# Seven half-size products for each third pair of up-projection tiles, and a feed-forward in three chunks

## The chip, the cores and the metric

The kernel runs on one core of a Trainium2 chip. The metric is the device time of one execution in microseconds (us). Five engines work side by side, each on its own list of instructions in a fixed order: TensorE (PE; its weight loads are shown as PEld), VectorE (DVE), ScalarE (ACT), GpSimd (POOL) and SyncE (SP, which here only issues transfers). An instruction whose operands aren't ready holds up all that stand behind it on its engine.

## The reference, cut to what matters

One step of a one-layer decoder for 512 prompt tokens and 64 sample tokens (576 columns in all); all is fp32. Retention and dilated attention share one input projection and one output projection; what the change touches is the feed-forward behind them:

```
h = _rmsnorm(x, norm2_w)
ua, ub = jnp.split(h @ w_up, [D_FF], axis=-1)          # 1024 -> 2 x 2816
buf = jnp.concatenate([conv_s0.astype(ua.dtype), ua], axis=1)
conv = conv_b
for j in range(CONV_W):                                 # 3 taps along the tokens
    conv = conv + buf[:, j:j + T] * conv_w[j]
x = x + (jax.nn.silu(conv) * ub) @ w_down               # 2816 -> 1024
```

## The kernel before, in words

Activations lie transposed: features on the 128 partitions, the 576 tokens along the free axis, worked on in two halves of 288 columns (`H2`). A weight tile is 128 output columns over 1024 inputs, that is eight blocks of 128 x 128.

Each fp32 operand is split in two parts of fp32r, hi and lo, and a product is hi x hi + hi x lo + lo x hi. So for each block `dense` issues three kinds of matmul on two halves: six matmuls of 288 columns. The weights' hi part is a ScalarE copy (`w_split_hi`, L219), the lo part a VectorE subtraction (`w_split_lo`, L229); both are made one tile ahead of TensorE. SyncE loads the raw tiles (L211), up to three in flight.

The feed-forward handles 22 pairs of tiles. Pair `f` is tile `f` of the first half of `w_up` (`ua`, the branch with the convolution) and tile `22 + f` (`ub`, the gate): 16 blocks, 96 matmuls. `up_post` then scales `ua` by the norm (L1130), does the convolution (ScalarE L1134, VectorE L1138 and L1139), SiLU (ScalarE L1141), scales `ub` (L1146), multiplies both (L1149, L1150, on GpSimd except at a half's last pair) and splits the result into `ghi` (L1152) and `glo` (L1154). After 11 pairs, `dense` takes their 11 results through the down projection: 8 output tiles, each summing over the 11 blocks in order, so the newest result is read last. Then the other 11 pairs and their down projection follow. `last_down` does the last output tile in two column parts (L1222), and `last_norm` follows.

The order on each engine is fixed when the kernel is built: streams of Python generators (`Merge`) are interleaved by the costs they yield. `up_post` is a stream of its own beside the stream of matmuls.

Of the kernel before, what the change touches and what calls it, by code (L numbers as in the profile page):

```python
# [18 lines left out]
P = 128  # L19
D = 1024  # L20
NP = 512
NS = 64
# [124 lines left out]
def decoder_step(ctx, tc, a):  # L147
# [33 lines left out]
    chunks = []  # L181
    IN_ORDER = [4 * sec + hp for hp in range(4) for sec in (1, 2, 0)]
    IN_ORDER += [4 * sec + hp for hp in range(4) for sec in (5, 4, 6)]
    IN_ORDER += [12 + hp for hp in range(4)]
    for m in IN_ORDER:
        chunks.append((("in", m, 0), a["w_in"], m, 0, 8))
    for m in range(8):
        chunks.append((("out", m, 0), a["w_out"], m, 0, 8))
    NFH = 11
    for half in range(2):  # L190
        for f in range(half * NFH, (half + 1) * NFH):
            chunks.append((("up", f, 0), a["w_up"], f, 0, 8))
            chunks.append((("up", NF + f, 0), a["w_up"], NF + f, 0, 8))
        for m in range(8):
            k0 = half * NFH
            chunks.append((("down", m, k0), a["w_down"], m, k0, k0 + 6))
            chunks.append((("down", m, k0 + 6), a["w_down"], m, k0 + 6, k0 + 11))
    raw, split = {}, {}
    state = {"load": 0, "use": 0}

    def w_load(upto):
        while state["load"] < min(upto, len(chunks)):
            w_load_part(state["load"], 0, 8)
            state["load"] += 1

    def w_load_part(i, c0, c1):
        _, w, m, k0, k1 = chunks[i]
        if i not in raw:
            raw[i] = wp.tile([P, 8, P], F32, name="wraw", tag="wraw", bufs=3)
        c1 = min(c1, k1 - k0)  # L210
        sp.dma_start(raw[i][:, c0:c1], wsrc(w, m, k0 + c0, k0 + c1))  # L211

    def w_split_hi(i, c0=0, c1=None):
        if i >= len(chunks) or i in split and c0 == 0:
            return
        if i not in split:
            split[i] = [wp.tile([P, 8, P], F32R, name="whi", tag="whi", bufs=2), None]
        c = slice(c0, c1 or chunks[i][4] - chunks[i][3])
        act.activation(split[i][0][:, c], raw[i][:, c], AF.Copy)  # L219

    def w_split_lo(i, c0=0, c1=None):
        if i >= len(chunks) or split[i][1] is not None and c0 == 0:
            return
        if split[i][1] is None:
            split[i][1] = wp.tile([P, 8, P], F32R, name="wlo", tag="wlo", bufs=2)
        hi, lo = split[i]
        n = chunks[i][4] - chunks[i][3]
        c = slice(c0, c1 or n)
        dve.tensor_sub(lo[:, c], raw[i][:, c], f32(hi[:, c]))  # L229
        if c.stop == n:  # L230
            raw.pop(i)

    def w_split(n):
        for i in range(state["use"], n):
            w_split_hi(i)
            w_split_lo(i)

    def w_next(key):
        i = state["use"]
        assert chunks[i][0] == key, (chunks[i][0], key)  # L240
        w_split(i + 1)
        state["use"] += 1
        return i, split.pop(i)

    def dense(ps, key, xhi, xlo, k0, k1, first, last, rows=None, made=None):

        i, (hi, lo) = w_next(key)
        w_split_hi(i + 1)
        for k in range(k0, k1):
            while made is not None and k not in made:  # L250
                yield None
            for wt, x in ((hi, xhi), (hi, xlo), (lo, xhi)):
                for s in range(2):
                    pe.matmul(ps[:, C0 + s * H2:C0 + (s + 1) * H2], wt[:, rows[k] if rows else k - k0], x[k][:, s * H2:(s + 1) * H2],  # L254
                              start=first and k == k0 and wt is hi and x is xhi,
                              stop=last and k == k1 - 1 and wt is lo)
            if k == k0 + 1:
                w_split_lo(i + 1)
            if k == k0 + 3:
                w_load(i + 4)  # L260
            yield 738.0, 0.0
# [167 lines left out]
    def w_first():  # L429
        for i, h in ((0, 0), (1, 0), (0, 1), (1, 1)):  # L430
            w_split_hi(i, 4 * h, 4 * h + 4)
            yield 0.0, 700.0
            w_split_lo(i, 4 * h, 4 * h + 4)
            wk.add((i, h))
            yield 0.0, 900.0
# [3 lines left out]
    def in_first():  # L439
# [5 lines left out]
        for _, _, i, k in steps:  # L445
            while k not in split_k or (i, k // 4) not in wk:
                yield None
            hi, lo = split[i]
            for wt, x in ((hi, xhis), (hi, xlos), (lo, xhis)):
                for s in range(2):  # L450
                    pe.matmul(ps[i][:, C0 + s * H2:C0 + (s + 1) * H2], wt[:, k], x[k][:, s * H2:(s + 1) * H2],  # L451
                              start=k == 0 and wt is hi and x is xhis, stop=k == KD - 1 and wt is lo)
            if k == KD - 1:
                state["use"] += 1
                split.pop(i)
                if i == 0:
                    w_split_hi(2)
                    w_split_lo(2)
# [7 lines left out]
        yield from dense(first[m], ("in", m, 0), xhis, xlos, 0, KD, True, True)  # L466
# [109 lines left out]
    def in_proj():  # L576
        for m in IN_ORDER:
# [3 lines left out]
            else:  # L581
# [3 lines left out]
                for c in dense(ps, ("in", m, 0), xhis, xlos, 0, KD, True, True):  # L585
# [440 lines left out]
    fp = ctx.enter_context(tc.tile_pool(name="ffn", bufs=1, reuse_waits="tile"))  # L1026
    hhi = fp.tile([P, KD, T], F32R, name="hhi")
    hlo = fp.tile([P, KD, T], F32R, name="hlo")
    hhis, hlos = [hhi[:, k] for k in range(KD)], [hlo[:, k] for k in range(KD)]
    acc = fp.tile([P, T], F32, name="acc")  # L1030
    csT = fp.tile([P, NF, 16], F32, name="csT")
    cout = fp.tile([P, 18, NF], F32, name="cout")
    nfw = fp.tile([P, D], F32, name="nfw")
    UE = NP + 2 + B * (TS + 2)
    ss2 = stat[:, 10:15]
# [3 lines left out]
    def sum_squares(m, norm):  # L1039
# [4 lines left out]
        sq = fp.tile([P, T], F32, name="sq", tag="sq", bufs=2)  # L1044
# [23 lines left out]
    h_made, norm2_made, cs_made, up_made, rows_made = set(), [], [], [], set()  # L1068
# [9 lines left out]
    def out_proj():  # L1078
        for m in range(KD):
            ps = dtile()  # L1080
            yield from dense(ps, ("out", m, 0), xhis, xlos, 0, KD, True, True, MIX)
            mg.add(out_post(m, ps))
        yield 0.0, 200.0

    def out_post(m, ps):
            dve.tensor_add(xT[:, m], tok(ps), xT[:, m])
            if m % 4 == 2:
                keep_rows()
            yield 0.0, 900.0
            act.activation(hhi[:, m], xT[:, m], AF.Copy, scale=n2[:, m:m + 1])  # L1090
            yield 0.0, 100.0
            dve.scalar_tensor_tensor(hlo[:, m], xT[:, m], n2[:, m:m + 1], f32(hhi[:, m]), op0=OP.mult,
                                     op1=OP.subtract)
            sum_squares(m, 2)
            h_made.add(m)
            if m == KD - 1:
                while len(h_made) < KD:
                    yield None
                yield 0.0, 3400.0
                yield from norm2()  # L1100
# [14 lines left out]
    def up(f, ghi, glo, made):  # L1115
        pa = dtile()
        yield from dense(pa, ("up", f, 0), hhis, hlos, 0, KD, True, True, made=h_made)
        pb = dtile()
        done = []
        mg.add(up_post(f, pa, pb, done, ghi, glo, made), None, 4000.0 if f == 0 else 0.0)  # L1120
        yield from dense(pb, ("up", NF + f, 0), hhis, hlos, 0, KD, True, True)
        done.append(1)

    def up_post(f, pa, pb, done, ghi, glo, made):
# [8 lines left out]
        c = fp.tile([P, UE], F32, name="cv", tag="cv", bufs=2)  # L1133
# [11 lines left out]
        g = fp.tile([P, T], F32, name="g", tag="g", bufs=2)  # L1145
        dve.tensor_mul(g, tok(pb), rstd_b)  # L1146
        yield 0.0, 1000.0
        eng = dve if f % NFH == NFH - 1 else pool
        eng.tensor_tensor(g[:, :NP], g[:, :NP], c[:, :NP], op=OP.mult)  # L1149
        eng.tensor_tensor(by_seq(g[:, NP:]), by_seq(g[:, NP:]), seqs(c, 0, TS), op=OP.mult)  # L1150
        yield 0.0, 3200.0 if eng is pool else 1000.0
        act.copy(ghi[f % NFH], g)  # L1152
        yield 0.0, 2300.0
        dve.tensor_sub(glo[f % NFH], g, f32(ghi[f % NFH]))  # L1154
        made.add(f % NFH)
        up_made.append(f)
        if f % 2 == 0:
            keep_rows()
# [16 lines left out]
    def rows_out(m, yn):  # L1175
        ps, p2 = mtile(), mtile()
        for j in range(5):
# [4 lines left out]
        dve.tensor_tensor(yn[:, 0:4, c], ps.rearrange("p (j c) -> p j c", j=4),  # L1182
                          nfw[:, None, c].to_broadcast([P, 4, P]), op=OP.mult)
        dve.tensor_tensor(yn[:NS, 4, c], p2[:NS, :P], nfw[:NS, c], op=OP.mult)
        rows_made.add(m)

    def g_tiles(which):
        t = big.tile([P, KD, T], F32R, name="b" + which, tag="b" + which, bufs=1)
        u = fp.tile([P, NFH - KD, T], F32R, name="g" + which, tag="g" + which)
        return [t[:, k] for k in range(KD)] + [u[:, k] for k in range(NFH - KD)]  # L1190

    def down_post(m, ps, half, yn):
        dve.tensor_add(xT[:, m], tok(ps), xT[:, m])
        if half == 1:
# [10 lines left out]
    def last_down(ghi, glo, yn):  # L1205

        m, k0 = KD - 1, NFH
# [4 lines left out]
        for p, (c, tiles) in enumerate(parts):  # L1212
            n = c.stop - c.start
            for k in range(NFH):
                if p == 0 and k in (0, 6):
                    i, (hi, lo) = w_next(("down", m, k0 + k))
                    w += [(hi[:, x], lo[:, x]) for x in range(min(6, NFH - k))]
                    if k == 0:
                        w_split_hi(i + 1)
# [112 lines left out]
```

## Time and profile before

| | us |
|---|---|
| median of 3 runs | 829.08 (828.67 to 830.43) |
| the profiled execution's own time | 830.02 |
| its span, first to last instruction | 828.2 |
| TensorE busy | 809.3 (98%) |
| VectorE busy | 413.4 (50%) |
| ScalarE busy | 294.4 (36%) |
| GpSimd busy | 148.0 (18%) |

The profile is of one execution; its own time stands 1.8 us above its span and 0.9 us above the median of the runs. A matmul's shown duration overlaps with that of the next, so how fast TensorE works is read from a long unbroken piece of the chain divided by its matmuls.

### The profile page before, as it was taken

To read this page: it belongs to the slowest core of one execution; us is meant where nothing else is said; L and a number is where in the kernel's file an instruction comes from. 1 tells how busy PE (TensorE), PEld (TensorE's weight loads), DVE (VectorE), ACT (ScalarE), POOL (GpSimd) and SP (SyncE) were. 2 spreads that over 40 slices of the span, in tenths; PEclk is the share of its full clock that TensorE was granted. 3 is DMA by queue.
4 is the path that set the end of the run, shared out by engine and by line. 5 is a ranking of instruction groups with operands and counts; after the bars stand their busy time and mean duration, and the time that the engine had idled before them with its cause. 6 is when DMAs were issued, how large, how long until landed. Compare 5 with 4: busy or idle time off the path is not lost.

```text
span 828.2 us, 15913 instructions
## 1 busy us (share of the span) xinstructions
PE 809.3 (98%) x6559; PEld 772.3 (93%) x6559; DVE 413.4 (50%) x792; ACT 294.4 (36%) x503; POOL 148.0 (18%) x240
## 2 busy tenths in 40 slices
PE   7999999999999999999999999999999999999995
PEld 5999999887887888999999999999999999999995
DVE  4664555665546566743545545432245545443333
ACT  5422222454535567433223323311123323332222
POOL 1321202111110213032122322100012322310111
PEclk9999999999999999999999999999999999999998
DMA  9354753678786863456255554443334455543213
GB/s 265 105 175 115 213 173 101 184 210 226 213 254 185 228 177 91 111 185 197 77 179 178 178 187 160 124 137 91 96 99 161 145 153 179 172 160 93 71 52 115
DMA packets 179798, 128.67 MB, mean 155 GB/s; under 512 B 14976, under 2 KB 176400, under 8 KB 179213
## 3 DMA queue, kind: packets, MB, share of 16 engines
q1 hardware_dynamic: 178573, 93.75, 40.4%
q10 hardware_dynamic: 928, 33.63, 11.3%
q8 instruction: 52, 0.85, 0.4%
q0 software_dynamic: 224, 0.28, 0.1%
q14 instruction: 21, 0.17, 0.1%
HBM read 121.52 MB, written 39.66 MB: 195 GB/s over the span
## 4 chain that ended last, share of the span: by engine, by line
PE 93%; ACT 3%; DVE 1%; issue 1%; DMA 1%; POOL 0%; SPq 0%; ACTq 0%; DVEq 0%
PE d L254 74%; PE m L883 2%; PE d L451 2%; PE m L928 1%; PE d L893 1%; PE m L810 1%; PE m L797 1%; PE m L496 1%; PE m L1222 1%; PE px L254 1%; PE m L666 1%; DMA wraw<-in_w_in_dram 1%; ACT s L786 1%; PE m L630 1%; PE px L410 1%
## 5 line engine op out<-in xcount | busy, mean ns | idle before, releaser
L219 ACT ACTIVATE whi<-wraw 128x1024 fp32r<-128x1024 f32 (+2 forms) x114 | 110.5, 970 | 369.2 <-issue 182.6
L229 DVE TENSOR_TENSOR wlo<-wraw,whi 128x1024 fp32r<-128x1024 f32 (+2 forms) x114 | 127.1, 1115 | 121.7 <-ACT whi L219 118.9
L254 PE MATMUL d<-bhi,whi 128*128 128x288 f32 x768 | 172.7, 306 | 1.2 <-DVE t L557 1.2
L254 PE MATMUL d<-bhi,wlo 128*128 128x288 f32 x768 | 164.2, 295 | 0.0
L254 PE MATMUL d<-blo,whi 128*128 128x288 f32 x768 | 163.9, 295 | 0.0
L254 PE MATMUL d<-hhi,whi 128*128 128x288 f32 x704 | 151.0, 296 | 0.0
L254 PE MATMUL d<-hlo,whi 128*128 128x288 f32 x704 | 150.8, 296 | 0.0
L254 PE MATMUL d<-hhi,wlo 128*128 128x288 f32 x704 | 150.7, 296 | 0.0
L254 PEld LDWEIGHTS d<-bhi,whi 128*128 128x128 f32 x768 | 121.7, 189 | 6.3 <-issue 3.1
L254 PEld LDWEIGHTS d<-bhi,wlo 128*128 128x128 f32 x768 | 123.3, 188 | 0.0
L254 PEld LDWEIGHTS d<-blo,whi 128*128 128x128 f32 x768 | 123.2, 188 | 0.0
L254 PEld LDWEIGHTS d<-hhi,whi 128*128 128x128 f32 x704 | 113.5, 189 | 0.1
L254 PEld LDWEIGHTS d<-hhi,wlo 128*128 128x128 f32 x704 | 113.5, 189 | 0.0
L254 PEld LDWEIGHTS d<-hlo,whi 128*128 128x128 f32 x704 | 113.5, 189 | 0.0
L1130 DVE TENSOR_TENSOR ue<-d,rstd_b 128x512 f32<-128x512 f32 x22 | 15.2, 691 | 74.5 <-PE d L254 74.5
L1149 POOL TENSOR_TENSOR g<-g,cv 128x512 f32<-128x512 f32 x20 | 25.8, 1289 | 142.2 <-DVE g L1146 136.7
L791 POOL TENSOR_SCALAR s<-s,sc 128x128 f32<-128x128 f32 (+3 forms) x32 | 17.3, 549 | 140.5 <-DVE sc L789 125.9
L1046 POOL TENSOR_TENSOR acc<-acc,sq 128x576 f32<-128x576 f32 x13 | 20.9, 1611 | 104.2 <-ACT sq L1045 104.2
L1135 POOL COPY cout<-ue 128x2 f32<-128x2 f32 x22 | 5.7, 260 | 137.6 <-DVE ue L1130 137.6
L884 ACT COPY kt<-m 128x384 f32<-128x384 f32 x32 | 15.3, 479 | 38.4 <-PE m L883 36.2
L883 PE MATMUL m<-ident,kc 128*128 128x128 f32 x192 | 27.4, 277 | 0.8 <-DVE sc L779 0.7
L884 DVE COPY kt<-m 128x384 f32<-128x384 f32 x32 | 17.8, 556 | 19.4 <-PE m L883 19.0
(269 smaller groups left out, 1027.3 us busy)
## 6 DMA issues: line engine op xcount, KB each, us to landing
wraw<-in_w_up_dram SPq DMA_DIRECT2D x44, 512.0 KB, 4.7
wraw<-in_w_in_dram SPq DMA_DIRECT2D x26, 512.0 KB, 3.8
kc<-in_cache_win_k_dram SPq DMA_DIRECT2D x32, 256.0 KB, 4.8
vc<-in_cache_win_v_dram SPq DMA_DIRECT2D x32, 256.0 KB, 3.2
wraw<-in_w_down_dram SPq DMA_DIRECT2D x16, 384.0 KB, 4.0
wraw<-in_w_down_dram SPq DMA_DIRECT2D x16, 320.0 KB, 3.2
kc<-in_cache_win_k_dram SPq DMA_DIRECT2D x64, 64.0 KB, 3.4
vc<-in_cache_win_v_dram SPq DMA_DIRECT2D x64, 64.0 KB, 3.3
```

Of the source, the lines that this page charges most:

```text
L219: act.activation(split[i][0][:, c], raw[i][:, c], AF.Copy)
L229: dve.tensor_sub(lo[:, c], raw[i][:, c], f32(hi[:, c]))
L254: pe.matmul(ps[:, C0 + s * H2:C0 + (s + 1) * H2], wt[:, rows[k] if rows else k - k0], x[k][:, s * H2:(s + 1) * H2], start=first and k == k ...
L410: pe.transpose(ps[:, s], xn[:r, j, k * P:(k + 1) * P], ident[:r, :r])
L451: pe.matmul(ps[i][:, C0 + s * H2:C0 + (s + 1) * H2], wt[:, k], x[k][:, s * H2:(s + 1) * H2], start=k == 0 and wt is hi and x is xhis, stop ...
L496: pe.transpose(p1[:, j * P:(j + 1) * P], src[:, j * P:(j + 1) * P], ident)
L791: pool.tensor_scalar(s[:, :n], s[:, :n], c[:, 2:3], 1.0, op0=OP.mult, op1=OP.mult)
L883: pe.transpose(ps[:, j * P:(j + 1) * P], K[u, x][:, 3 * w + j], ident)
L884: (act.copy if w else dve.tensor_copy)(kt[:, w * 384:w * 384 + 384], ps[:, :384])
L1046: pool.tensor_tensor(acc, acc, sq, op=OP.add)
L1130: dve.tensor_mul(u[:, 2:NP + 2], ya[:, :NP], rstd_b[:, :NP])
L1149: eng.tensor_tensor(g[:, :NP], g[:, :NP], c[:, :NP], op=OP.mult)
```

## The change

Of the 22 pairs, seven (`f` = 2, 5, 8, 11, 14, 17, 20) are now done as a product of 2 x 2 blocks in Winograd's form of Strassen's scheme: the weights' block rows are `ua` and `ub` and their block columns are inputs 0 to 511 and 512 to 1023, the activations' blocks are those two input halves by the two token halves. Seven products of 4 blocks by 288 columns take the place of eight: 7 x 4 x 3 = 84 matmuls for 96.

The activations' sums T1 to T4 are made and split once, in `out_post`, beside the output projection, whose tiles come in the order 0, 4, 1, 5 ... for that. The weights' sums S1 to S4 are made on VectorE for each of the seven pairs, from four quarters ahead (`sums`), and each is split like a weight. The products' results are put together on VectorE with copies that ScalarE takes out of PSUM (`ct`, `g`).

Weights are now split in quarters of a pair (up to four blocks), two to three quarters ahead, not a tile at a time; the next raw tile is loaded when one is used up. The feed-forward goes in three chunks of 6, 8 and 8 pairs, each followed by its part of the down projection. GpSimd's part in the gate goes to VectorE for all pairs. The final norm's weight is loaded behind the last pair.

```diff
-    NFH = 11
-    for half in range(2):
-        for f in range(half * NFH, (half + 1) * NFH):
-            chunks.append((("up", f, 0), a["w_up"], f, 0, 8))
-            chunks.append((("up", NF + f, 0), a["w_up"], NF + f, 0, 8))
+    CHUNKS = [(0, 6), (6, 14), (14, 22)]
+    SEVEN = set(range(2, NF - 1, 3))
...
+    def add_slab(f):
...
+        quarters.extend([(i, slice(0, 4)), ("S1", f), (i, slice(4, 8)), ("S2", f), ("S4", f), (i + 1, slice(4, 8)),
+                         ("S3", f)])
+        reads[i], reads[i + 1] = 5, 3
+        for n, which in ((-4, "S1"), (-3, "S2"), (-2, "S4"), (-1, "S3")):
+            sums.setdefault(j + n, []).append((which, f, i))
...
+    def ahead_of():
+        return 3 if state["ffn"] else 2
+    def w_begin(j):
+        for which in sums.pop(j, []):
+            w_sum(*which)
+        while state["hi"] <= min(j + ahead_of(), len(quarters) - 1):
+            if state["lo"] < state["hi"]:
+                w_lo(state["lo"])
+                state["lo"] += 1
+            w_hi(state["hi"])
+            state["hi"] += 1
...
+    def up_seven(f, n, ghi, glo, made):
...
+        order = ((pa, "B11"), (pc, "T1"), (pb, "B21"), (pa, "T2"), (pc, "B22"), (pd, "T4"), (pa, "T3"))
+        for q, (dst, c) in enumerate(order):
...
+            for k in range(4):
+                while c[0] == "T" and (c, k) not in t_made:
+                    yield None
+                for wt, b in ((hi, xh), (hi, xl), (lo, xh)):
+                    pe.matmul(dst, wt[:, k], b[:, k], start=q in (0, 1, 2, 5) and k == 0 and wt is hi and b is xh,
+                              stop=k == 3 and wt is lo, skip_group_check=True)
...
+            if q == 0:
+                act.copy(ts[0], pa)
+            elif q == 1:
+                act.copy(ts[1], pc)
+            elif q == 2:
+                dve.tensor_tensor(y[:, :H2], pb, ts[0], op=OP.add)
+            elif q == 3:
+                act.copy(ts[2], pa)
+            elif q == 4:
+                dve.tensor_tensor(y[:, H2:T], pc, ts[2], op=OP.add)
+                mg.add(post_seven(f, n, pa, ts[1], y, z, stage, ghi, glo, made))
+            elif q == 5:
+                act.copy(z[:, :H2], pd)
...
+    def post_seven(f, n, pa, t, y, z, stage, ghi, glo, made):
...
+        dve.tensor_mul(u[:, 2:NP + 2], y[:, :NP], rstd_b[:, :NP])
...
+        act.activation(c[:, :L], u[:, 0:L], AF.Identity, scale=convw[:, 0, f:f + 1], bias=convb[:, f:f + 1])
...
+        dve.tensor_tensor(z[:, :H2], pa, z[:, :H2], op=OP.add)
+        dve.tensor_tensor(z[:, H2:T], pa, t, op=OP.add)
+        yield 0.0, 900.0
+        dve.scalar_tensor_tensor(c[:, :L], u[:, 1:L + 1], convw[:, 1, f:f + 1], c[:, :L], op0=OP.mult, op1=OP.add)
+        dve.scalar_tensor_tensor(c[:, :L], u[:, 2:L + 2], convw[:, 2, f:f + 1], c[:, :L], op0=OP.mult, op1=OP.add)
...
+        dve.tensor_mul(z[:, :T], z[:, :T], rstd_b)
...
+        yield from gated(f, n, z, c, ghi, glo, made)
```

The two orders on TensorE. In the up projection before, in any pair: each weight block serves the two token halves, in two PSUM banks.

```order
L254 MATMUL d<-hhi,whi 128x288 x2
L254 MATMUL d<-hlo,whi 128x288 x2
L254 MATMUL d<-hhi,wlo 128x288 x2
L254 MATMUL d<-hhi,whi 128x288 x2
L254 MATMUL d<-hlo,whi 128x288 x2
```

Now, in one of the seven pairs, at the end of its first product and in its second (`T` is a sum of activations):

```order
L1262 MATMUL m<-hhi,whi 128x288
L1262 MATMUL m<-hlo,whi 128x288
L1262 MATMUL m<-hhi,wlo 128x288
L1262 MATMUL m<-T,whi 128x288 x2
L1262 MATMUL m<-T,wlo 128x288
L1262 MATMUL m<-T,whi 128x288 x2
```

The 288-column matmuls stand in groups of three to one bank now, not of six to two; 12 fewer of them make up a pair.

VectorE's order where the first chunk of the feed-forward ends and its down projection begins. Before, from the `ub` of pair 10, the last of its half, to the first output tile of the down projection:

```order
L1146 TENSOR_TENSOR g<-d,rstd_b 128x576
L1149 TENSOR_TENSOR g<-g,cv 128x512
L1150 TENSOR_TENSOR g<-g,cv 128x64
L229 TENSOR_TENSOR wlo<-wraw,whi 128x768
L1154 TENSOR_TENSOR glo<-g,ghi 128x576
L1193 TENSOR_TENSOR xT<-d,xT 128x576
```

Now, from where the last product of pair 5, the last of its chunk, can be read (L1295) to the first output tile (L1377); two splits of weights, not shown, stand right ahead:

```order
L1295 TENSOR_TENSOR g<-m,g 128x288
L1296 TENSOR_TENSOR g<-m,ct 128x288
L296 TENSOR_TENSOR wlo<-wraw,whi 128x384
L1298 SCALAR_TENSOR_TENSOR cv<-ue_4471,vec,cv 128x592
L1299 SCALAR_TENSOR_TENSOR cv<-ue_4471,vec,cv 128x592
L1302 TENSOR_TENSOR g<-g,rstd_b 128x576
L1308 TENSOR_TENSOR g<-g,cv 128x512
L1309 TENSOR_TENSOR g<-g,cv 128x64
L1313 TENSOR_TENSOR blo<-g,bhi 128x576
L296 TENSOR_TENSOR wlob<-wraw,whib 128x384
L1377 TENSOR_TENSOR xT<-d,xT 128x576
```

Between the last matmul of the chunk's last pair and its last result (`glo`, `blo`) stood five instructions; now nine stand there, and the pair's two convolution steps are among them.

## Rows read from the trace of the kernel before

**Rows 1.** The page's head and its part 1: busy time.
```profile
span 828.2 us, 15913 instructions
PE 809.3 (98%) x6559; PEld 772.3 (93%) x6559; DVE 413.4 (50%) x792; ACT 294.4 (36%) x503; POOL 148.0 (18%) x240
```

**Rows 2.** Busy time by stretch (us; then PE, PEld, DVE, ACT, POOL, granted clock, DMA).
```profile
440.00:480.00 40.00, 40.00 (x302) 40.00 (x301) 18.57 (x24) 12.79 (x16) 9.40 (x15) 1.00 0.55 172
800.00:828.00 28.00, 19.47 (x148) 18.61 (x146) 9.22 (x27) 7.15 (x10) 3.12 (x3) 0.90 0.23 85
```

**Rows 3.** The chain that ended last, in order of time (start us, us, what).
```profile
400.18 349.44 PE d L254 x2622
...
809.59 1.76 PE m L1222 x12
...
816.78 2.16 PE m L1222 x18
```

**Rows 4.** Groups of VectorE by form, 340 to 828 us (busy us, mean ns | idle before).
```profile
L229 DVE TENSOR_TENSOR wlo<-wraw,whi 128x1024 fp32r<-128x1024 f32 x51 | 62.5, 1225 | 64.6 <-ACT whi L219 62.6
...
L1138 DVE SCALAR_TENSOR_TENSOR cv<-ue,vec,cv 128x592 f32<-128x592 f32 x22 | 18.1, 823 | 0.0
L1146 DVE TENSOR_TENSOR g<-d,rstd_b 128x576 f32<-128x576 f32 x22 | 16.5, 750 | 0.0
...
L1130 DVE TENSOR_TENSOR ue<-d,rstd_b 128x512 f32<-128x512 f32 x22 | 15.2, 691 | 74.5 <-PE d L254 74.5
...
L1131 DVE TENSOR_TENSOR ue<-d,rstd_b 128x64 f32<-128x64 f32 x22 | 4.7, 214 | 0.0
...
L1237 DVE TENSOR_TENSOR xT<-m,xT 128x320 f32<-128x320 f32 x1 | 0.5, 490 | 3.6 <-PE m L1222 3.6
...
L1237 DVE TENSOR_TENSOR xT<-m,xT 128x256 f32<-128x256 f32 x1 | 0.4, 425 | 0.8 <-PE m L1222 0.8
```

**Rows 5.** Groups by form over the whole span: the smallest splits.
```profile
L229 DVE TENSOR_TENSOR wlo<-wraw,whi 128x512 fp32r<-128x512 f32 x4 | 2.8, 688 | 2.9 <-ACT whi L219 2.9
...
L219 ACT ACTIVATE whi<-wraw 128x512 fp32r<-128x512 f32 x4 | 2.5, 631 | 5.8 <-DMA wraw<-in_w_in_dram 5.8
```

**Rows 6.** Groups of ScalarE by form, 340 to 828 us.
```profile
L219 ACT ACTIVATE whi<-wraw 128x1024 fp32r<-128x1024 f32 x51 | 54.0, 1060 | 207.1 <-issue 150.2 <-PE d L254 56.8
L1134 ACT ACTIVATE cv<-ue,vec 128x592 f32<-128x592 f32 x22 | 19.4, 880 | 5.7 <-DVE ue L1131 5.5
L1141 ACT ACTIVATE cv<-cv 128x592 f32<-128x592 f32 x22 | 15.0, 683 | 2.9 <-DVE cv L1139 2.9
...
L1152 ACT CAST bhi<-g 128x576 fp32r<-128x576 f32 x16 | 10.5, 657 | 0.0
...
L1283 ACT ACT_TABLE_LOAD x1 | 1.3, 1283 | 0.0
```

**Rows 7.** Timeline of VectorE in one pair (start us, us, line).
```profile
449.62 0.75 DVE L1154 TENSOR_TENSOR blo<-g,bhi 128x576 fp32r<-128x576 f32 x1
450.29 0.82 DVE L1138 SCALAR_TENSOR_TENSOR cv<-ue,vec,cv 128x592 f32<-128x592 f32 x1
```

**Rows 8.** Timeline of ScalarE in the same pair.
```profile
448.35 0.66 ACT L1152 CAST bhi<-g 128x576 fp32r<-128x576 f32 x1
448.91 0.88 ACT L1134 ACTIVATE cv<-ue,vec 128x592 f32<-128x592 f32 x1
```

**Rows 9.** Timeline of VectorE and TensorE where the first down projection begins.
```profile
537.13 0.75 DVE L1154 TENSOR_TENSOR glo<-g,ghi 128x576 fp32r<-128x576 f32 x1
...
538.57 0.43 PE L254 MATMUL d<-ghi,whi 128*128 128x288 f32 x2
```

**Rows 10.** Timeline of TensorE, first matmuls of the span.
```profile
9.92 0.85 PE L451 MATMUL d<-blo,whi 128*128 128x288 f32 x2
...
14.93 0.42 PE L451 MATMUL d<-blo,whi 128*128 128x288 f32 x2
```

**Rows 11.** Busy time by stretch, columns as in rows 2: the end of the span.
```profile
822.00:824.00 2.00, 0.00 (x0) 0.00 (x0) 0.92 (x2) 1.15 (x1) 0.00 (x0) 0.65 0.81 217
```

More of the change, by code (lines that the diff above doesn't have):

```diff
@@ L233, in w_split, with w_read @@
[L233 to L261, printed above, removed]
+    def w_read(i):
+        reads[i] -= 1
+        if not reads[i]:
+            raw.pop(i)
+        if state["auto"]:
+            while state["load"] < len(raws) and len(raw) < (4 if state["ffn"] else 3):
+                w_load(state["load"] + 1)
@@ new lines, in w_hi, with w_lo @@
+    def w_hi(j):
+        if j < len(quarters) and j not in split:
+            src = w_src(j)
+            n = src.shape[1]
+            split[j] = [w_tile("whi", j), None]
+            act.activation(split[j][0][:, :n], src, AF.Copy)
+    def w_lo(j):
+        if j < len(quarters) and split[j][1] is None:
+            src = w_src(j)
+            n = src.shape[1]
+            split[j][1] = w_tile("wlo", j)
+            dve.tensor_sub(split[j][1][:, :n], src, f32(split[j][0][:, :n]))
+            x, c = quarters[j]
+            if isinstance(x, str):
+                S.pop((x, c))
+                if x == "S3":
+                    w_read(quarters[keys["seven", c]][0] + 1)
+            else:
+                w_read(x)
@@ new lines, in dense @@
+    def dense(ps, key, xhi, xlo, k0, k1, first, last, made=None):
+        j, k = keys[key], k0
+        while k < k1:
+            w_begin(j)
+            if split[j][1] is None:
+                w_mid(j)
+            hi, lo = split.pop(j)
+            c = quarters[j][1]
+            for x in range(c.stop - c.start):
+                while made is not None and k not in made:
+                    yield None
+                for wt, b in ((hi, xhi), (hi, xlo), (lo, xhi)):
+                    for s in range(2):
+                        pe.matmul(ps[:, C0 + s * H2:C0 + (s + 1) * H2], wt[:, x],
+                                  b[k][:, s * H2:(s + 1) * H2],
+                                  start=first and k == k0 and wt is hi and b is xhi,
+                                  stop=last and k == k1 - 1 and wt is lo)
+                if x == 0:
+                    w_mid(j)
+                k += 1
+                yield 738.0, 0.0
+            j += 1
@@ L1144, in up_post @@
         yield 0.0, 1400.0
-        g = fp.tile([P, T], F32, name="g", tag="g", bufs=2)
-        dve.tensor_mul(g, tok(pb), rstd_b)
+        g = tmp("g")
+        dve.tensor_mul(g[:, :T], tok(pb), rstd_b)
         yield 0.0, 1000.0
[L1148 to L1158, printed above, removed]
+        yield from gated(f, n, g, c, ghi, glo, made)
     def conv_state_out():
@@ L1290, in feed_forward @@
                 ps = dtile()
[L1291 to L1294 removed]
+                yield from dense(ps, ("down", m, f0), ghi, glo, 0, f1 - f0, True, True, made=made)
+                mg.add(down_post(m, ps, last, yn))
     mg.add(conv_state_in(), None)
```

314 lines of the change are left out of this document (209 added, 105 removed).

## The prediction

> **What bounds the kernel now.** I read the page's head first: TensorE is busy for 809.3 of 828.2 us, VectorE for half the span [rows 1]. Of the 18.9 us that are left, 8.5 us lie in the last 28 us, where little but the final norm is left to do [rows 2]; 10.4 us are all the rest, the start of the span included. The chain of waits then has one unbroken piece of 349.44 us of nothing but the matmuls of `dense`, from the first pairs through the first down projection to the second [rows 3]. So in the feed-forward TensorE is the limit: a matmul less is time off the kernel, and any moment for which TensorE waits is time on it. In a middle stretch of 40 us of it VectorE works 18.57 us and ScalarE 12.79 us [rows 2]; both have room, VectorE less.
>
> **What a matmul costs.** 349.44 us over 2622 matmuls is 133.3 ns for 288 columns [rows 3]. The new order writes one PSUM bank at a time, with hi, hi, lo of a block behind each other. That pattern is there already, in `last_down`: 12 matmuls of 320 columns in 1.76 us (147 ns) and 18 of 256 in 2.16 us (120 ns) [rows 3]. Half-way between lies 133.3 ns, so I take the same price. Taken away are 7 x 12 = 84 matmuls: **-11.2 us**.
>
> **What VectorE and ScalarE get on top.** A split of 512 elements takes VectorE 688 ns against 1225 ns for one of 1024 [rows 4, 5], ScalarE 631 against 1060 ns [rows 5, 6]. Sums of weights are not in the trace; the nearest row is the 512-element subtraction, which reads two tiles in SBUF too, so 688 ns. An addition of 288 columns out of PSUM lies between 425 ns (256) and 490 ns (320) [rows 4]: 457 ns. For ScalarE's copies of 288 columns I take 440 ns, from 631 ns less 224 elements at the slope of its two splits.
>
> A pair of the old kind then costs VectorE 4 splits (2.75), the scaling of `ua` (0.69 + 0.21), two convolution steps (0.82 each), the scaling of `ub` (0.75), the gate (about 0.69 + 0.21, as the scaling of `ua` has these shapes) and `glo` (0.75): 7.7 us beside 12.8 us of TensorE. One of the seven costs 7 splits (4.82), 4 sums (2.75), 4 half additions (1.83) and the same 4.95 us: 14.35 us beside 84 x 0.1333 = 11.2 us. Alone it is too much; over two old and one new it is 29.8 us in 36.8 us. All hangs on whether the surplus can move to the neighbours.
>
> I walked the order of both engines through such pairs, each instruction starting when its engine and its operands are free. Operations that don't depend on each other overlap by about 0.08 us on VectorE (450.29 is less than 449.62 + 0.75) and 0.1 us on ScalarE (448.91 is less than 448.35 + 0.66) [rows 7, 8]. Weights are split three quarters ahead, 4.8 us of these products. In pair 2, where the activations' sums have delayed VectorE most (it gets to the scaling of pair 1's `ua` 1.3 us late), the walk has every split ready over 2 us before its matmul; in the other pairs over 1.7 us. The copies out of `pa`, which must end before TensorE adds to it again, come about 2 us early. So between the pairs I cost all this at **0**; if the cover were gone, the first to be late would be the lo part of a product's weights, and each microsecond of it would be one on the chain.
>
> The split T sums (32 half-size operations on VectorE, some 15 us) lie beside the output projection and pairs 0 and 1, 77 us of TensorE: **0**. In front of the feed-forward the quarter splits add 26 x 0.15 us on VectorE and 26 x 0.2 us on ScalarE in 330 us, but let ScalarE wait less for TensorE's buffers; of TensorE's matmuls there the order is unchanged. I take **0**, with bounds of 2 us each way, a fifth of the 10.4 us of idle time. Eight more additions to `xT` for the third down projection (750 ns each at most) lie beside 6 blocks of matmuls each: 0. The final norm's weight, now loaded late, has 6.4 us of matmuls as cover.
>
> **The new wait.** The down projection reads the newest pair last. Before, pair 10 stood behind ten others: `glo` ended at 537.88 and its first matmuls began at 538.57 [rows 9], 0.7 us to spare. The first chunk has 6 pairs, so its newest result is due after 5 blocks of 6 matmuls, 4.0 us, and that pair, 5, is one of the seven: everything behind its last product starts only then. My walk, in us from the start of its first product; the last one ends at 11.2, readable at 11.4:
>
> ScalarE: cast of pair 4 5.9 to 6.5, hi of S3 to 7.1, copy of `pa` to 7.4, two hi parts for down (384 elements, 0.52 each) to 8.3, `cv` (after the scaled `ua`) 10.6 to 11.5, copy of `pd` to 11.8, three more hi parts to 13.1.
> VectorE: lo of S3 7.1 to 7.8, `glo` of pair 4 to 8.5, a lo part (384, 0.55) to 8.9, second `y` addition to 9.3, lo to 9.8, scaled `ua` to 10.6, two lo parts 12.3 to 13.3, two `z` additions to 14.1, lo to 14.5, convolution to 16.2 (its second step waits for the first), scaling of `z` to 16.8, gate 16.9 to 17.7; ScalarE's cast to 18.4; `glo` 18.45 to 19.2.
>
> TensorE would have begun this block at 15.2 and needed `glo` two matmuls later, at 15.47: it waits **3.8 us**. Bounds: were nothing else in the queues, from 11.4 on two additions, convolution, scaling, gate, cast and `glo` end at 17.0, a wait of 1.5 us; with every duration in full and no overlap the walk ends at 21.0, a wait of 5.5 us. I take 3.8, as rows 7 and 8 show the overlap. VectorE's section on the drain in the Trainium skill (VectorE: DVE Perf Modes, "The DRAIN you can't avoid") has an operation start only when the pipe behind the one before is empty, unless it isn't held; by its first half the time would be that of the 5.5 us, and the overlap in rows 7 speaks for its second.
>
> The second chunk ends with two old pairs: the same walk has its last `glo` 3.9 us behind the last matmul, due after 7 blocks, 5.6 us. The third ends with an old pair behind a new one, with two table loads of ScalarE (1.28 us each [rows 6]) in the way: 5.5 us, due at 5.6 us. Both **0** (bound 1.2 us for the third).
>
> **Sum.** 828.2 - 11.2 + 3.8 = 820.8 us of span; 830.02 - 7.4 = 822.6 us for the profiled execution, whose own time is 0.94 us above the median of the runs, so **821.7 us** for the median. The gap's bounds give 819.4 to 823.4; the front's 2 us and the third end's 1.2 us widen that to 817.4 to 826.6.
>
> **Rivals.**
> *VectorE becomes the bound (slower).* If the surplus of each new pair can't move, TensorE waits in each for 14.35 - 11.2 = 3.2 us: 7 x 3.2 = 22 us, 829.1 - 11.2 + 22 + 3.8 = 843.7 us; with the overlap of 0.08 us on 20 operations it is 1.55 us each, 832.6 us. It decides from waits of (11.2 - 3.8) / 7 = 1.06 us per pair on. For it: 14.35 against 11.2 us, and a VectorE that waits in order for copies and products. Against it: 29.8 in 36.8 us over three pairs, and sums that start four quarters ahead. Chance 0.11.
> *The clock falls in the wait (824 to 826 us).* In 822 to 824 us, with no matmul running, the granted clock's mean is 0.65 of the 2.4 GHz, which is a fall to the lower level of 1.2 GHz on the way [rows 11]; behind the idle start two matmuls took 0.85 us against 0.42 us later, from 9.9 to some time before 14.9 us [rows 10]. At half pace for 5 to 9 us, TensorE would lose 2.5 to 4.5 us. Our wait of 3.8 us is the only one that long. The Trainium skill (TensorE: Matmul & The Clock Gate, "HAM oscillation — how this bites in real kernels") says that TensorE is throttled again in such idle gaps between matmuls; by that rule the time would be this rival's. The trace shows it only where all work was over. Chance 0.12.
> *The products run slower.* If a change of weights at each third matmul cost more than shown, 588 matmuls at 146 ns would eat all (89.6 - 3.8 = 85.8 us over 588). Rows 3 stand against it: at 256 columns the same pattern runs at 120 ns. Chance 0.03, some 829 us.
> *No wait at the first chunk's end, or a faster front (816 to 818.5 us).* Chance 0.06.
>
> My forecast has the remaining 0.68. Range 818 to 826.5 us. A measurement of this kernel tells about 0.2% (1.7 us) from no change: faster 0.85, within 0.07, slower 0.08, the last from the first and third rivals.
>
> **What would show it.** TensorE's matmuls of `up_seven`: 588, in unbroken pieces at 133 ns, 11.2 us a pair. One idle gap of 2 to 5 us on TensorE, ended by ScalarE's cast or VectorE's `blo`, some 4 us behind the end of pair 5; none above 1 us at the ends of the other chunks. VectorE busy for over 60% between the first new pair and the last. I am wrong if TensorE waits for `wlo` in several of the seven pairs, if the pace within them is not 133 ns, or if the clock drops behind the gap.

## The result, and the profile after

| | before | after |
|---|---|---|
| median of 6 runs each, us | 829.69 (828.67 to 831.05) | 840.09 (839.43 to 845.11) |
| after / before, 95% interval | | 1.0142 (1.011 to 1.0174) |
| span of the profiled execution, us | 828.2 | 843.2 |
| mean granted clock of TensorE in it | 0.997 | 0.985 |

The change made the kernel slower by 10.4 us where 7.4 us less were forecast. The profiled execution took 845.11 us at a granted clock of 0.985, as two of the six do; the other four took 839.4 to 840.1 us at 0.989. So what is read from the profile below holds for an execution 5 us above the median.

The head of the page after, with busy time and the granted clock in 40 slices, answers to [rows 1]:

```profile
span 843.2 us, 16199 instructions
PE 806.4 (96%) x6475; PEld 767.5 (91%) x6475; DVE 504.2 (60%) x1064; ACT 338.7 (40%) x670; POOL 100.8 (12%) x200
PEclk9999999999999999999999989999999999999997
```

TensorE is busy for 2.9 us less than before, not 11.2, and idle for 36.8 us instead of 18.9. So there are two things to find: 18 us of new waits, and 8.3 us by which the same matmuls ran slower.

Who TensorE waited for, over the whole span (us in total, times, longest):

```profile
PE px L486 <- DMA vrows<-in_norm_w_dram: 5.5, 1, 5.5
PE m L883 <- POOL s L877: 4.7, 4, 2.7
PE d L337 <- ACT bhi L1311: 3.2, 1, 3.2
PE d L337 <- DVE t L643: 2.6, 1, 2.6
PE m L969 <- DVE sc L865: 2.3, 3, 1.3
PE m L1148 <- POOL acc L1141: 2.1, 1, 2.1
PE d L337 <- DVE g L1341: 1.6, 1, 1.6
PE d L979 <- DVE t L649: 1.3, 1, 1.3
```

The first row is the start, as before. L1311 is the gap at the first chunk's end, forecast at 3.8 us; L1141 and L1341 stand at the feed-forward's beginning. All the others (`s`, `t`, `sc`: operations of the attention) lie in front of it, from 150 to 350 us, where TensorE's waits add up to 13.4 us against 4.0 before. That part of the program was forecast at 0.

A landmark shows the same: the squares of the output projection's columns (ScalarE). Before, and after:

```profile
L1045 ACT ACTIVATE sq<-xT x7: 669/673/674, 350.8 to 389.5; 128x576 f32<-128x576 f32 x7
```

```profile
L1140 ACT ACTIVATE sq<-xT x7: 666/669/672, 367.6 to 409.5; 128x576 f32<-128x576 f32 x7
```

They begin 16.8 us later than before and end 20 us later.

The granted clock, by stretch (columns as in [rows 2]):

```profile
168.80:172.20 3.40, 3.40 (x24) 1.50 (x17) 1.21 (x3) 0.00 (x0) 0.00 (x0) 0.50 0.61 159
...
243.90:247.30 3.40, 3.40 (x18) 3.38 (x17) 0.56 (x1) 0.67 (x2) 0.52 (x4) 0.50 0.56 143
271.20:274.60 3.40, 3.21 (x14) 3.04 (x15) 1.46 (x5) 0.65 (x2) 0.48 (x2) 0.50 0.18 53
489.60:496.40 6.80, 5.91 (x23) 5.62 (x24) 2.58 (x5) 1.62 (x3) 0.00 (x0) 0.50 0.28 80
```

Four stretches at 1.2 instead of 2.4 GHz, 17 us in all, each at or behind one of the longer waits: 17 / 2 = 8.5 us, about the 8.3 us that busy TensorE lost. Before, there was none between the start and the end of the work.

The new pairs themselves, and the first chunk's end, in the chain of waits, in order of time:

```profile
435.71 11.10 PE m L1262 x84
446.82 25.41 PE d L337 x192
472.23 10.99 PE m L1262 x83
...
489.76 0.68 ACT bhi L1311
...
490.49 62.77 PE d L337 x450
553.26 11.14 PE m L1262 x84
```

Seven times 84 matmuls in 11.1 us, with nothing between them and their neighbours: this part is as forecast. VectorE's last result of pair 5 comes behind the cast:

```profile
490.47 0.76 DVE L1313 TENSOR_TENSOR blo<-g,bhi 128x576 fp32r<-128x576 f32 x1 [0.74 <-ACT bhi L1311]
```

**The account of the profiled execution**, from the forecast span of 820.8 us: waits in front of the feed-forward 13.4 - 4.0 = 9.4; three half-clock stretches there 3 x 1.7 = 5.1; 1.9 us in the first 18 us, where two matmuls took 0.68 us and more until 18.1 us (before, 0.42 us at 14.9 us [rows 10]), by the lines below; two waits at the feed-forward's beginning 3.7; half clock behind the gap 3.4; the gap 3.2 instead of 3.8. That is 843.7; the span is 843.2 us.

The same matmuls near the start, before and after:

```profile
16.25 0.80 PE L410 MATMUL px<-ident,xn 128*128 128x128 f32 x5
```

```profile
17.66 0.68 PE L535 MATMUL d<-bhi,wlo 128*128 128x288 f32 x2
18.14 1.03 PE L494 MATMUL px<-ident,xn 128*128 128x128 f32 x5
```

### The profile page after: what moved, and what is told of

The parts are those of the page before. It is cut to its first block, busy times and chain, and to the rows that moved or that the text cites. A ratio compares the mean times of both kernels' runs of the same rounds, so it can differ in the third digit from the quotient of the medians.

```text
span 843.2 us, 16199 instructions
## 1 busy us (share of the span) xinstructions
PE 806.4 (96%) x6475; PEld 767.5 (91%) x6475; DVE 504.2 (60%) x1064; ACT 338.7 (40%) x670; POOL 100.8 (12%) x200
## 3 DMA queue, kind: packets, MB, share of 16 engines
q10 hardware_dynamic: 928, 33.63, 11.1%
## 4 chain that ended last, share of the span: by engine, by line
PE 48%; DVE 1%; ACT 1%; issue 0%; POOL 0%; ACTq 0%; DVEq 0%; POOLq 0%
PE d L337 37%; PE m L1262 9%; PE m L1407 1%; PE m L1364 0%; ACT yn L1453 0%; DVE wlo L296 0%; PE m L1387 0%; POOL acc L1141 0%; PE m L1148 0%; DVE T L1184 0%; ACT whi L289 0%; ACT cv L1329 0%; DVE cv L1299 0%; DVE yn L1448 0%; DVE g L1341 0%
## 5 line engine op out<-in xcount | busy, mean ns | idle before, releaser
L296 DVE TENSOR_TENSOR wlo<-wraw,whi 128x512 fp32r<-128x512 f32 (+1 forms) x149 | 107.8, 729 | 88.7 <-ACT whi L289 87.8
L337 PEld LDWEIGHTS d<-bhi,whi 128*128 128x128 f32 x784 | 125.8, 191 | 11.1 <-ACT bhi L1311 3.4
L289 ACT ACTIVATE whi<-wraw 128x512 fp32r<-128x512 f32 (+1 forms) x149 | 90.3, 619 | 70.0 <-PE d L337 47.3
L337 PE MATMUL d<-hhi,whi 128*128 128x288 f32 x400 | 85.2, 294 | 1.6 <-DVE g L1341 1.6
L337 PE MATMUL d<-hlo,whi 128*128 128x288 f32 x400 | 85.4, 295 | 0.0
L337 PE MATMUL d<-hhi,wlo 128*128 128x288 f32 x400 | 85.3, 294 | 0.0
L337 PEld LDWEIGHTS d<-hhi,whi 128*128 128x128 f32 x400 | 63.9, 188 | 1.9 <-ACT whi L289 1.8
L337 PEld LDWEIGHTS d<-hhi,wlo 128*128 128x128 f32 x400 | 63.9, 188 | 0.0
L337 PEld LDWEIGHTS d<-hlo,whi 128*128 128x128 f32 x400 | 63.7, 187 | 0.0
L1377 DVE TENSOR_TENSOR xT<-d,xT 128x576 f32<-128x576 f32 x23 | 17.4, 757 | 39.9 <-PE d L337 39.9
L1262 PE MATMUL m<-T,whi 128*128 128x288 f32 x168 | 33.9, 295 | 0.0
L1330 POOL COPY cout<-ue 128x2 f32<-128x2 f32 x15 | 11.1, 739 | 185.4 <-DVE ue L1325 185.4
L1311 ACT CAST bhi<-g 128x576 fp32r<-128x576 f32 x22 | 14.8, 674 | 44.3 <-DVE g L1309 44.3
L1141 POOL TENSOR_TENSOR acc<-acc,sq 128x576 f32<-128x576 f32 x13 | 19.3, 1487 | 102.7 <-ACT sq L1140 102.7
```

The lines of the kernel that those rows point to most:

```text
L289: act.activation(split[j][0][:, :n], src, AF.Copy)
L296: dve.tensor_sub(split[j][1][:, :n], src, f32(split[j][0][:, :n]))
L337: pe.matmul(ps[:, C0 + s * H2:C0 + (s + 1) * H2], wt[:, x], b[k][:, s * H2:(s + 1) * H2], start=first and k == k0 and wt is hi and b is xh ...
L1141: pool.tensor_tensor(acc, acc, sq, op=OP.add)
L1262: pe.matmul(dst, wt[:, k], b[:, k], start=q in (0, 1, 2, 5) and k == 0 and wt is hi and b is xh, stop=k == 3 and wt is lo, skip_group_chec ...
L1311: act.copy(ghi[n], g[:, :T])
```

## The theory, and its rivals

**Why the front is late.** The attention's operations on VectorE are not slower (`t` takes 0.75 us in both traces); they stand behind something. Who VectorE waited for from 150 to 345 us, as to `wlo`, the weights' lo part. Before:

```profile
DVE wlo L229 <- ACT whi L219: 2.0, 3, 0.8
```

After:

```profile
DVE wlo L296 <- ACT whi L289: 14.7, 15, 1.6
```

One of the fifteen, in the timelines of ScalarE, VectorE and TensorE:

```profile
166.31 0.63 ACT L289 ACTIVATE whi<-wraw 128x512 fp32r<-128x512 f32 x1
...
166.97 0.69 DVE L296 TENSOR_TENSOR wlo<-wraw,whi 128x512 fp32r<-128x512 f32 x1 [1.61 <-ACT whi L289]
167.58 0.75 DVE L649 TENSOR_TENSOR t<-d,rstd_b 128x576 f32<-128x576 f32 x1
...
168.39 1.60 PE L979 MATMUL d<-kt,qb 128*32 128x512 f32 x8 [1.33 <-DVE t L649]
```

ScalarE comes to `whi` only behind four casts of the attention. VectorE reaches `wlo` 1.61 us too early and stands; `t`, whose operands are ready, stands behind it; TensorE waits 1.33 us for `t`, and the clock falls. Before, hi and lo of a tile were issued at a dense's start and behind its second block; after, the lo part follows one block behind its hi part, and there are twice as many.

Theory A: the distance of lo from hi in the queues (A1 in experiment 2). Rivals: the number of splits (B); the hi parts' place on ScalarE (A2). For the rest: the gap of 3.2 us comes of a new pair read last, and the clock falls because of the gap; the two waits at the feed-forward's beginning come of the T sums and of the added copy in `out_post`.

## The experiments

All times are medians of device time; the kernel before has 829.6 to 830.1 us beside them.

**1. Both parts in the places of before** (`front_order`)

```diff
     def w_begin(j):
...
-        while state["hi"] <= min(j + ahead_of(), len(quarters) - 1):
-            if state["lo"] < state["hi"]:
+        if not state["ffn"] and j % 2:
+            return
+        while state["hi"] <= min(j + 3, len(quarters) - 1):
+            if state["ffn"] and state["lo"] < state["hi"]:
...
-                if x == 0:
+                if x == (0 if state["ffn"] else 1):
                     w_mid(j)
...
```

> In front of the feed-forward the half-size weight splits are issued in the places of before (both hi parts at a dense's start, both lo parts behind its second block); all else is the changed kernel. Theory A (the new places of the splits in ScalarE's and VectorE's queues make the attention part late): the feed-forward starts within 5 us of before instead of 17 us behind it, TensorE's waits from 150 to 350 us fall from 13.4 us to under 6 us, and with them most of the three 3.4 us stretches at half clock go; 840.1 - 9 - 4 = about 827 us (824 to 831). Rival B (it is the number of splits, twice as many, whatever their place): waits stay over 10 us, 837 to 841 us. The gap at the first chunk's end stays 3.2 us in both.

Measured: 831.4 us, ratio 1.001 (0.9997 to 1.0024), just above the expected 824 to 831 us. The first square starts at 351.0 us (before 350.8), the waits from 150 to 350 us are 3.9 us, and no half-clock stretch is left in front. Run again beside experiment 10:

> The kernel with the splits in front in the places of before once more, beside the filled gap: 831.4 us (829.5 to 832.5) with a gap of 3.1 us near 475 us and a stretch of 3.4 or 6.8 us at half clock behind it.

Measured: 829.5 us, ratio 1.0003 (0.9991 to 1.0015), gap 3.13 us, 3.4 us at half clock from 475.5 us. B is out: there are as many splits as in the changed kernel.

**2. The lo parts alone** (`front_lo_later`)

```diff
-                if x == 0:
+                if x == (0 if state["ffn"] else 2):
                     w_mid(j)
```

> The changed kernel with one thing moved: in front of the feed-forward VectorE's lo parts are issued behind the third block of a half instead of behind the first; ScalarE's hi parts stay where the change has them, a half at a time. Theory A1 (VectorE, which works in order, stands at a lo part until ScalarE has made the hi part issued just before it, 14.7 us in 15 waits from 150 to 345 us, and the attention's work stands behind it): these waits go, TensorE's waits in 150 to 350 us fall from 13.4 to under 5 us, and the time comes to that of the run with both parts in the places of before, 831 us (829 to 833). Theory A2 (the hi parts' new place on ScalarE does as much): TensorE still waits for 7 us or more there, 835 to 840 us.

Measured: 831.6 us, 1.001 (0.9998 to 1.0023); TensorE's waits from 150 to 350 us 4.6 us, and of VectorE's waits from 150 to 345 us this is left:

```profile
DVE wlo L296 <- ACT whi L289: 0.9, 2, 0.5
```

A1 holds: two blocks more between hi and lo give 8.5 us back. ScalarE's order needs no change.

**3. Chunks that end with an old pair** (`chunks_7_7_8`)

```diff
-    CHUNKS = [(0, 6), (6, 14), (14, 22)]
+    CHUNKS = [(0, 7), (7, 14), (14, 22)]
```

> Chunks (0,7), (7,14), (14,22) in place of (0,6), (6,14), (14,22), so that each ends with a pair of the old kind; all else is the changed kernel. Theory A (the gap comes of a new pair read last, and the clock falls because of the gap): no wait over 1 us at the first chunk's end and no half-clock stretch behind it; 840.1 - 3.2 - 3.4 = 833.5 us. Rival B (the clock falls for another reason): the 6.8 us at half clock stay, 836.9 us. Rival C (the next-to-last pair being new only moves the wait): 839 to 841 us.

Measured: 836.8 us, 1.0086 (1.0064 to 1.0107). The time is the one that rival B gave; the trace speaks for A: no wait stands between 428 and 820 us, and no half clock. The gain of 3.3 us is half of what was expected from the profiled execution; that most runs of the changed kernel had less half clock to give back may be why (0.989 against 0.985 of 840 us is an estimated 3.4 us, which would leave the gap's own 3.2 us). Where the clock fell in those runs isn't seen.

**4. Both** (`front_order_chunks_7_7_8`)

> Both edits at once. If they act in different places their gains add: about 827 - 6.6 = 820.5 us (817 to 825), faster than before by about 1%. Rival: with the front early again another engine or a transfer is late in the feed-forward; over 828 us.

Measured: 825.8 us, 0.9942 (0.9921 to 0.9964). The gains add (831.4 - 825.8 = 5.6, and 836.8 - 825.8 = 11.0 us), but the median is above the expected range: the waits of 2.1 and 1.6 us at the feed-forward's beginning are still there, with 3.4 us at half clock between them.

**5. No pair by seven products, no T sums** (`no_seven_no_sums`)

```diff
-    SEVEN = set(range(2, NF - 1, 3))
+    SEVEN = set()
...
-        h1 = hs.pop(k)
...
-        yield from h_split("T3", k, b12)
+        hs.pop(k)
```

> No pair by the seven products (all 22 pairs by dense) and none of the T sums; splits by halves, leads, chunks and gate are those of the changed kernel. Leaves nothing out of the result. Theory A (the seven products save 84 matmuls at 133 ns as forecast, 11.2 us, and the T sums cost the 3.7 us of waits in the first two pairs, and the gap with its half clock needs a new pair at the chunk's end): 840.1 + 11.2 - 3.7 - 6.6 = 841 us, waits in front of the feed-forward as in the changed kernel. Rival B (the new pairs or the T sums are what made it slower): 830 us or less.

Measured: 843.3 us, 1.0152 (1.0125 to 1.0179). The waits in front are those of the changed kernel (the same rows, the same 2.7 and 2.6 us); from 350 to 830 us TensorE never waits. So neither the products nor their sums made the front late, and both waits at the feed-forward's beginning go with the sums. The added copy in `out_post` is still in this kernel, so by itself it makes neither wait. Its feed-forward pays the 84 matmuls back: 840.1 + 11.2 - 3.7 - 3.2 - 1.7 (a half-clock stretch of 3.4 us) = 842.7.

**6. Squares first** (`squares_first`, on 4)

```diff
+        sum_squares(m, 2)
         h = hs[m] = tmp("h")
         act.activation(hhi[:, m], xT[:, m], AF.Copy, scale=n2[:, m:m + 1])
         act.activation(h[:, :T], xT[:, m], AF.Copy, scale=n2[:, m:m + 1])
...
         h_made.add(m)
-        sum_squares(m, 2)
```

> The kernel with the splits in the places of before and chunks of 7, 7, 8, and in it ScalarE's square for the norm's sum issued ahead of the two scaled copies of a column instead of behind them. Theory (the added fp32 copy of 0.76 us, with the other ahead of it, makes GpSimd's last addition and so the sums on TensorE late): the wait of 2.06 us for GpSimd's addition near 397 us falls to about 0.6 us, and the 3.4 us at half clock behind it may go: 825.8 - 1.5 = 824.3, without the half clock 822.6 us. Rival (VectorE's late residual addition sets it): the wait stays above 1.5 us, 825 to 826 us.

Measured: 820.0 us, **0.9869 (0.9853 to 0.9886)**. The wait for GpSimd's addition is gone, and the half clock. The gain, 5.8 us, is more than the 2.1 + 1.7 us of these two; in the two profiled executions full clock came at 10.6 instead of 17.0 us, which is another 3 us, and whether that is so in the other runs isn't seen. The rival has a share: counted from the feed-forward's first matmul (389.55 us in 4, 386.59 us here), GpSimd's last addition begins 2.5 us earlier, 1.3 us of it by the square's new place and 1.2 us because VectorE's last residual addition (`xT`) is earlier. In 4 that stood behind a lo part that waited 0.94 us for its hi part and took 1.56 us:

```profile
391.46 1.56 DVE L296 TENSOR_TENSOR wlo<-wraw,whi 128x512 fp32r<-128x512 f32 x1 [0.94 <-ACT whi L289]
392.95 0.74 DVE L1190 TENSOR_TENSOR xT<-d,xT 128x576 f32<-128x576 f32 x1
```

**7. T sums ahead of the norm** (`sums_before_norm`, on 6)

```diff
-            yield 0.0, 3400.0
-            yield from norm2()
+            mg.add(norm2(), None, 3400.0)
```

> As the run with the squares first, and the last T sums are issued ahead of the norm's short operations instead of behind them. Theory (the T sums behind the norm delay the scaling of the first pair's two products, so TensorE waits 1.57 us for a free PSUM tile): that wait goes, 821 to 823 us. Rival (they now delay the norm itself): a wait of 1 us or more for the broadcast of the norm's factors, no gain.

Measured: 820.5 us, 0.9881 (0.9858 to 0.9904). The rival: the wait of 1.57 us for `g` became one of 1.59 us for the norm's factors (`stat`).

**8. T sums behind the first gate's scaling** (`sums_after_first_gate`, on 6)

```diff
             yield from norm2()
+            while not first_g:
+                yield None
...
-    ues = []
+    first_g, ues = [], []
...
         dve.tensor_mul(g[:, :T], tok(pb), rstd_b)
+        first_g.append(1)
```

> As the run with the squares first (820 us), and the last column pair's T sums wait until VectorE has scaled the first pair's second product. Theory (the 1.57 us wait for that scaling near 409 us comes of the T sums and splits ahead of it in VectorE's queue): the wait goes, 818.4 us (817.5 to 819.5). Rival (the sums then come too late for the first product that needs them): TensorE waits for T near 418 us instead, 820 us or more.

Measured: 819.6 us, **0.9874 (0.9858 to 0.9891)**, the lowest median of all, at the upper end of what was expected (817.5 to 819.5). TensorE's longest waits now:

```profile
PE px L488 <- DMA vrows<-in_norm_w_dram: 4.9, 1, 4.9
PE d L537 <- ACT bhi L474: 1.5, 1, 1.5
PE m L1392 <- ACT sq L1430: 1.2, 1, 1.2
PE d L339 <- DVE t L645: 1.2, 1, 1.2
```

Two of the start, one of the end, and one in the attention that was there before; from 350 to 800 us none. Against squares first the median is 0.4 us lower, which the runs do not tell apart.

**9. Nine pairs instead of seven** (`nine_of_22_pairs`, on 7)

```diff
-    SEVEN = set(range(2, NF - 1, 3))
+    SEVEN = {2, 4, 7, 9, 11, 14, 16, 18, 20}
```

> As the run with the T sums ahead of the norm, with 9 pairs by seven products (2, 4, 7, 9, 11, 14, 16, 18, 20) instead of 7: 24 matmuls fewer. Two pairs in turn cost VectorE 14.35 + 7.7 = 22.05 us beside 24 us of TensorE. Theory (VectorE isn't the bound yet): 3.2 us less than with 7 pairs, about 818.5 us, no waits over 0.5 us in the new pairs. Rival (VectorE is the bound as soon as there is no third pair to take the surplus): TensorE waits for lo parts in most of the nine, 822 us or more.

Measured: 822.5 us, 0.9892 (0.9873 to 0.9912): 24 matmuls fewer, and a median 2.0 us above that with seven, which four runs each (820.8 to 822.9 and 819.7 to 823.3 us) don't tell apart. The 3.2 us that were to be saved did not come. The chain of waits from the end of pair 7 to the last products of pair 11 no longer runs through TensorE:

```profile
523.52 10.99 PE m L1263 x83
...
536.40 0.60 DVE wlob L296
...
554.47 0.70 DVE wlo L296
555.19 8.88 DMA wraw<-in_w_up_dram
...
577.94 0.39 ACT ct L1269
...
578.37 6.81 PE m L1263 x48
```

It goes through VectorE's splits, sums and convolutions, ScalarE, and one load that starts when VectorE frees its buffer. VectorE is busy for 43.4 of the 62 us from 523 us, so it is the order and not the sum that binds there. TensorE's waits are 2.4 us longer in all and the clock is half for 3.4 us; the rest of the loss isn't accounted for. The rival gave the time but not the mechanism: TensorE waits over 0.3 us in one of the nine pairs only (1.7 us, for `ct`), and for no weights' lo part longer than 0.2 us. That VectorE is the bound with every second pair is not shown.

**10. The gap filled with matmuls** (`gap_filled`, on 1)

```diff
...
+            c, b0 = quarters[j][1], xhi
...
+                if made is not None and spare and k == 5:
+                    d = spare.pop()
+                    for _ in range(24):
+                        pe.matmul(d[:, C0:C0 + H2], hi[:, x], b0[0][:, :H2], start=True, stop=True)
                 while made is not None and k not in made:
                     yield None
...
+                if f0 == m == 0:
+                    spare.append(dtile())
```

> The kernel with the splits in front in the places of before (chunks 6, 8, 8, so with the gap of 3.1 us at the first chunk's end), and in the gap 24 matmuls of 288 columns into a PSUM tile that nobody reads, ahead of the block that waits. The result is unchanged. Theory (the clock falls because TensorE stands idle in the gap): idle time there under 0.6 us, no stretch at half clock near 476 us, 1.7 to 3.4 us less than the same kernel without them in this call (831.4 us in the call before): 828 to 830 us. Rival (the clock falls whatever TensorE does there): a half-clock stretch of 3.4 us or more stays, the time is unchanged.

Measured: 829.0 us beside 829.5 us without them, a difference that these runs don't tell from none. What tells is the clock. The kernel without them (`front_order_again`), by stretch:

```profile
470.00:475.00 5.00, 2.47 (x19) 2.23 (x17) 4.71 (x9) 1.02 (x3) 0.00 (x0) 1.00 0.84 228
475.00:480.00 5.00, 4.40 (x20) 4.11 (x21) 2.45 (x4) 1.49 (x3) 0.00 (x0) 0.66 0.31 90
```

With them:

```profile
470.00:475.00 5.00, 5.00 (x40) 5.00 (x39) 4.47 (x8) 1.92 (x5) 0.00 (x0) 1.00 0.54 151
475.00:480.00 5.00, 4.74 (x34) 4.29 (x34) 3.28 (x6) 1.68 (x4) 0.00 (x0) 1.00 0.47 133
```

The block that waits does not start earlier, but what stands behind it runs at full pace. So in these traces the idle gap is what lowers the clock. Of the twelve runs with the matmuls seven had a granted clock of 0.993 to 0.996, where all twelve without them had 0.989 to 0.992; five had 0.990 or 0.991, and no trace shows where the clock fell in those. The Trainium skill (TensorE: Matmul & The Clock Gate, "HAM oscillation — how this bites in real kernels") has TensorE throttled again in idle gaps between matmuls; by that rule half clock behind a gap like the forecast one was to be expected, and these rows agree in kind.

## Why the prediction was wrong, step by step

- **"In front of the feed-forward ... I take 0, with bounds of 2 us each way": the step that failed.** It cost 14.5 us in the profiled run (9.4 of waits, 5.1 of clock); 8.5 us of median come back with experiment 2 alone, 12.6 us between the two profiled executions (843.2 and 830.6 us). The step added up the durations of the new operations and noted that TensorE's order is the same, but did not walk VectorE's and ScalarE's queues there, as it did in the feed-forward. TensorE's order says nothing when VectorE's has changed: each lo part had come one block behind its hi part. Nor would a total have told: over the whole span VectorE waited 118.9 us for hi parts before (the releaser in [rows 4] shows over half of it), almost all where nothing was behind the wait that mattered.
- **"The split T sums ... 0": wrong by 3.7 us** and, in the traces of experiments 1, 2, 4 and 10, a half-clock stretch of 3.4 us. They have 77 us of cover on average, but the last column's norm and the first pair's scaling are a chain in which each operation ahead counts. Without the sums neither wait is there (experiment 5). The first goes by ScalarE's order too (experiment 6), the second by the sums' place alone (experiment 8).
- **The clock's fall in the wait was a rival with 0.12, and its mechanism came true**, with 6.8 us at half clock in the profiled run (3.4 us of time; 2.5 to 4.5 forecast) and in experiment 2, 3.4 us in experiment 1 and its repetition. That the wait of 3.8 us would be "the only one that long" was not so: waits of 2.6 and 2.7 us in front lowered the clock as well. Experiment 10 shows the cause.
- **The new wait at the first chunk's end: right.** 3.19 us against 3.8 (bounds 1.5 to 5.5; the walk's own times give 19.2 - 15.47 = 3.7), ended by ScalarE's cast. From the end of the last product to the end of `glo` (`blo` in the trace) the walk gave 8.0 us (11.2 to 19.2); from 483.22 to 491.23 us it is 8.0. The walk's cast ends at 18.4, 3.2 us behind the block's due time of 15.2, as measured. A second wait, for `glo` itself, doesn't show because the block's first matmuls ran at half clock; with the gap filled (experiment 10) it is 0.26 us.
- **The price of a matmul and the saving: right.** 84 in 11.10 to 11.14 us, 132.4 ns against 133.3.
- **No waits between the pairs, none at the second and third chunk's end, none new at the tail: right**, with VectorE busy for 269 of 425 us (63%) from 390 us on. The first rival (VectorE the bound) did not happen; with nine such pairs VectorE's order reached TensorE in one of them (experiment 9).
- With the front, the chunks and the norm's beginning mended, the same seven products give 819.6 us, 2.1 us under the forecast of 821.7. That forecast holds 3.8 us for the gap, which these chunks don't have; without it 817.9 us was forecast, 1.7 us less than measured. So most of what had been forecast was in the change, and what had been costed at 0 ate it.

## What to carry to other kernels

Where an in-order engine waits for another's result, what counts is how far ahead in that engine's queue the result stands, and what is queued behind the wait: a lo part issued one block behind its hi part, where two or three blocks are enough, cost this kernel 8.5 us in a part that the change was not about. So walk the queues in every stretch in which an order changed, also where the bounding engine's own order is the same. And price a wait of TensorE at more than its length: here one of 3.2 us brought 3.4 or 6.8 us at half clock with it.

## What the runs showed of the hardware

- **VectorE against GpSimd.** A lo split of 512 elements takes 0.69 us. In the changed kernel eleven of them stand beside GpSimd's additions to `acc`, begin after these and take 1.38 to 1.83 us. One of the eleven, by the timelines of GpSimd and VectorE:

```profile
405.46 1.44 POOL L1141 TENSOR_TENSOR acc<-acc,sq 128x576 f32<-128x576 f32 x1 [7.01 <-ACT sq L1140]
...
405.87 1.57 DVE L296 TENSOR_TENSOR wlo<-wraw,whi 128x512 fp32r<-128x512 f32 x1 [0.94 <-ACT whi L289]
407.36 0.74 DVE L1188 TENSOR_TENSOR xT<-d,xT 128x576 f32<-128x576 f32 x1
408.03 0.67 DVE L296 TENSOR_TENSOR wlo<-wraw,whi 128x512 fp32r<-128x512 f32 x1
```

  The split ends 0.54 us behind GpSimd's addition (0.54 to 0.55 us in all eleven), as if it had waited for its end; the next one, with GpSimd idle, takes 0.67 us. The Trainium skill (SBUF — State Buffer, "Who interferes with whom") has a VectorE instruction with two SBUF inputs contend with a GpSimd instruction that reads SBUF, the later one blocked; these rows agree. In the kernel before, the later one was mostly GpSimd's addition: it took 1.82 us instead of 1.43 us where a VectorE operation on two SBUF tiles had begun 0.28 us earlier.
- **Which waits lower the clock.** Waits of 2.6 to 3.2 us did in each trace. One of 2.1 us did in experiments 1, 2, 4 and 10 (half clock from 397.4 us in the first) and did not in the changed kernel (411.75 us) or in experiment 3. One of 1.6 us did in experiment 9 (400.85 us, half clock from 401.8 us) and did not in 6 and 7. Those of 1.2 us by themselves never did. Two of 1.3 us within 4 us did in the changed kernel (165.6 and 168.4 us) and in experiment 5, and did not in experiment 3 (162.5 and 165.3 us); there one of 1.28 us (ended at 174.5 us, with 0.3 us more at 175.5 us) did, with half clock from 176.4 us. So the length of a wait alone doesn't tell it. The stretches were 3.4 or 6.8 us long.
- **The start.** Full clock came between 10.6 (experiment 6) and 18.6 us (the changed kernel) after the first instruction in the traces of these kernels, whose first matmuls are the same, so up to 4 us of an execution's time is decided there.
